# Wider products with v in a two-layer streaming encoder, with embedding products kept in memory meanwhile and first weights split two blocks ahead

## The chip, the core and the metric

The kernel runs on one core of a Trainium2 chip. The metric is the time of one execution on the device in microseconds (us); the median of several runs is compared. The core has a matrix engine (TensorE, "PE" in the profile, with "PEld" for its weight loads), a vector engine (VectorE, "DVE"), a scalar engine (ScalarE, "ACT"), a general engine (GpSimd, "POOL") and a queue that issues transfers (SyncE, "SP"). Each works through its own instructions strictly in the order written. TensorE writes its results to a small memory of accumulators, PSUM; the other data lie in the on-chip memory SBUF, and inputs and outputs lie in the chip's large memory.

## What is computed

Two request groups, 512 prompt frames and 32 sample frames, run through the same two layers; the kernel lays them side by side as 544 columns. Per layer:

```python
u = x @ w_in                       # 13 pieces: q,k,v,z of branch A; q,k,v,z of B; x,z of C; 3 gates
ya = band_attention(qa, ka, va)    # softmax over the frame's chunk of 64 and up to 8 chunks before it
yb = retention(rope(qb), rope(kb), vb); yc = rg_lru(conv(xr))
merged = sum of sigmoid(g_b) * ((y_b * silu(z_b)) @ w_branch[b]) over the three branches
r = ALPHA * x + merged @ w_out
r = r + sigmoid(r @ w_ple_gate) * (pe @ w_ple)     # pe: per-layer embedding input
x = layer_norm(r)
```

Two pieces matter here. In the attention of branch A, with 8 heads of 64 features, the softmax weights of a head are multiplied by v. And `pe @ w_ple`, called the embedding products below, is needed only at the end of a layer.

## The kernel before

Everything is feature-major: 128 features on the partitions, 544 frames along the free dimension, four such tiles in one "slab" of SBUF. There are 15 slabs in a pool that all large intermediate results share, and a slab that is free again is given to the next tile that asks for one.

**Weights in blocks.** A unit is a 128-feature slice of one product, such as `("pl", 3)` or `("wo", 0)`; it consists of 2, 4 or 8 blocks of 128 x 128 weights. `UNITS` (line 60) lists them in the order they run: the embedding products `pl` first, then x of the convolution, v, q and k of attention, the pieces of retention, the three branches, then `wo` (w_out) and `pg` (w_ple_gate). Numbers are kept at full precision by splitting each operand in a high and a low part: ACT copies a weight tile to a rounded high part (`split`, L209) and DVE subtracts to get the low part (L210). A block (L254) is then three products, high x high, high x low, low x high, each over 288 and 256 columns: six matmuls.

**The order of work.** The program is one list per engine, written out by hand. Each block is preceded by a `tick`, which raises a clock by one, calls `stream()` and lets waiting jobs (generators that yield a number of ticks) take their next step. `stream(lead)` splits the weights of all blocks up to `lead` blocks ahead of the present one, four blocks at a time; each second split of a chunk of eight blocks frees a landing buffer (there are three) and issues the load of a later chunk on the SP queue (L201). At the very start two transfers bring the embedding input, four the input x; ACT and DVE split them (`hilo`, L262 and L263). PE runs dummy products (`busy(WARM)`, L269) until its first operands are there. `evac` takes the accumulators of a unit to SBUF; for `pl` this is one ACT copy of 544 columns (L931) into a slab, `env["ple", 0]` or `env["ple", 1]`. Two accumulators serve all units in turn (`ps_mm`), so a unit can start only when the copy of the unit two before it is done.

**Attention of the prompt.** Heads go in pairs; a pair `p` takes three steps, `qs` = (0,1), (2,) and (3,), where each number is a block of 128 queries, which sees i+1 blocks of keys. `attn_step` first calls `flush()`, which issues the products with v that earlier steps left in `env["pvs"]`, then the scores (L402), the exponentials (L353 on DVE, L355 on ACT) and their division by the sum (L359, L360), then transposes the result on PE (L418) block by block and copies it back over itself (L419, ACT). Last it leaves its own product with v for a later flush. `attn_pv` (L432) has one product per block of queries, block of keys and head: 64 rows of output, 128 columns. A step begins every 8 ticks and ends 14 ticks after its start. The output of a pair goes to `ya` by a DVE copy (L437).

**End of a layer.** `gate` (L951 to L954) multiplies the sigmoid of the `pg` product by the embedding product, which has lain in its two slabs since the start of the layer. In the first layer `split_ahead` meanwhile splits weights of the second into slabs of their own.

Of the kernel before, what the change touches and what calls it, by code (L numbers as in the profile page):

```python
# [64 lines left out]
LEAD = 8  # L65

HELD = (6, 2)
WARM = 16

PACE = {  # L70
# [53 lines left out]
def encoder(ctx: ExitStack, tc, xT, pT, W, RB, KC, VC, PAR, CST, LGB, o_y, o_k, o_v, o_rp, o_rs, o_cv, o_lr):  # L124
# [9 lines left out]
    sm = pool("sm", 6)  # L134
    qs = pool("qs", 1)
    PS = bass.MemoryType.PSUM
    ps_mm = pool("ps_mm", 2, space=PS)
    ps_sc = pool("ps_sc", 2, space=PS)
    ps_tp = pool("ps_tp", 1, space=PS)
# [32 lines left out]

    def tick():
        clock[0] += 1
        stream()
        for j in list(jobs):
            while j[1] <= clock[0]:
                d = next(j[0], None)
                if d is None:
                    jobs.remove(j)  # L180
                    break
                j[1] = clock[0] + d
# [98 lines left out]

    def ple_split(l):
        pr, p2 = ple_in[l]
        for k in range(2):
            hilo(p2[:, k], p2[:, 2 + k], pr[:, k])

    V.memset(zero.bitcast(F32), 0.0)
    busy(WARM)
# [32 lines left out]
    def layer(l, env, nxt):  # L321
# [40 lines left out]
        def attn_job():  # L362
            while not all(k in env for k in ("vatok", "gates", ("K", 0))):
                yield 2
            env["ya"] = sl("ya")
            env["pvs"] = []
            bias_loads(0)
            yield 4
            for p in range(4):
                while ("K", p) not in env:  # L370
                    yield 2
                for j in range(2):
                    G.memset(env["bias", p, j][0:64, 448:512], NEG)
                for qs in ((0, 1), (2,), (3,)):
                    if qs[0] == 2 and p < 3:
                        bias_loads(p + 1)
                    add(attn_step(p, qs))
                    yield PACE["step"]
            yield PACE["attn_end"]
            flush()  # L380
            env["ya1"] = True
# [6 lines left out]
        def attn_step(p, qs):  # L388
            QTh, QTl, KTh, KTl = (env[k] for k in ("QTh", "QTl", "KTh", "KTl"))
            flush()  # L390
            scs, xs, todo = [psum("sc") for _ in range(2)], [], []
            o = 0
            now = [], []

            for j in range(2):
                xs.append(tmp("sx", (128, 512)))
            for i in qs:
                n = (i + 1) * 128
                for k, (q_, k_) in enumerate(((QTh, KTh), (QTl, KTh), (QTh, KTl))):
                    for j in range(2):  # L400
                        r = slice(64 * j, 64 * j + 64)
                        T.matmul(scs[j][:, o:o + n], lhsT=q_[r, p, i * 128:i * 128 + 128], rhs=k_[r, p, :n],  # L402
                                 start=k == 0, stop=k == 2)
                for j in range(2):
                    now[j].append((xs[j][:, o:o + n], scs[j][:, o:o + n], env["bias", p, j][:, 512 - n:]))
                o += n
            for j in range(2):
                for a in todo:
                    norm(*a)
                todo = [exps(*a) for a in now[j]]  # L410
                yield PACE["at1"]
            for a in todo:
                norm(*a)
            yield PACE["at2"]
            for j in range(2):
                tp = psum("tp")
                for c in range(0, o, 128):
                    T.transpose(tp[:, c:c + 128], xs[j][:, c:c + 128], ident)  # L418
                copy("p%d" % j)(xs[j][:, :o], tp[:, :o])  # L419
                yield PACE["at3"]  # L420
            env["pvs"].append(lambda: attn_pv(p, qs, xs))

        def attn_pv(p, qs, xs):
            if qs[0] == 0:
                env["pv"] = psum("pv")
            pv = env["pv"]
            o = 0
            for i in qs:
                for kt in range(i + 1):
                    for j in range(2):  # L430
                        h = 2 * p + j
                        T.matmul(pv[64 * j:64 * j + 64, i * 128:i * 128 + 128],  # L432
                                 lhsT=env["vatok"][:, kt, h * 64:h * 64 + 64], rhs=xs[j][:, o:o + 128],
                                 start=kt == 0, stop=kt == i)
                    o += 128
            if qs[-1] == 3:
                copy("pv")(env["ya"][:, p, :NP], pv)  # L437

        def sample_loads():
            t = sl("kvc", shape=(128, 4 * N))  # L440
# [404 lines left out]
        def evac(kind, t, ps, hf=None):  # L845
# [36 lines left out]
            elif kind == "xr":  # L882
                if t == 0:
                    env["xrp"] = xrp = sl("xrp", shape=(128, 4, N + 6))
                    V.memset(xrp[:, :, 0:3], 0.0)
                    V.tensor_copy(xrp[:, :, NP + 3:NP + 6], pa[:, P_SC:P_SC + 12].rearrange("p (a b) -> p a b", a=4))
                xrp = env["xrp"]
                S.copy(xrp[:, t, 3:3 + NP], pv[:, :NP])
                S.copy(xrp[:, t, NP + 6:], pv[:, NP:])  # L889
                if t == 3:  # L890
                    Q.dma_start(out=o_cv[l, :, :, 0:3], in_=xrp[:, :, NP:NP + 3])
                    Q.dma_start(out=o_cv[l, :, :, 3:6], in_=xrp[:, :, NP + NS + 3:NP + NS + 6])
                add(lru_tile(t), PACE["lt00"] if t == 1 else PACE["lt0"])
            elif kind in ("za", "zb", "zc"):
                for f in {"za": ("ya1", "ya2"), "zb": ("yb",), "zc": ("yc",)}[kind]:
                    need(env, f)
                y = env["y" + kind[1]]
                if t == 0:
                    env[kind] = (sl(kind + "h", F32R), sl(kind + "l", F32R))
                h, lo = env[kind]  # L900
                z = tmp("z")
                S.activation(z, pv, AF.Sigmoid)  # L902
                if kind == "zb":
                    V.scalar_tensor_tensor(z, pv, pcol(P_GN, t), z, MUL, MUL)
                else:
                    V.tensor_tensor(z, pv, z, MUL)
                V.tensor_tensor(z, z, y[:, t], MUL)
                hilo(h[:, t], lo[:, t], z)
            elif kind[0] == "g":
                sg = tmp("sg")  # L910
                S.activation(sg, pv, AF.Sigmoid)  # L911
                env["sg", t] = sg
            elif kind[0] == "b":
                sg = env.pop(("sg", t))
                a, b = t // 4, t % 4
                if kind == "bC":
                    if b == 0:
                        env["m", a] = sl("m")
                    V.tensor_tensor(env["m", a][:, b], pv, sg, MUL)
                else:  # L920
                    V.tensor_tensor(sg, pv, sg, MUL)  # L921
                    m = env["m", a][:, b]
                    (V if kind == "bB" and t == 7 else G).tensor_tensor(m, m, sg, ADD)  # L923
                    if kind == "bB":
                        if b == 0:
                            env["mh", a], env["ml", a] = sl("mh", F32R), sl("ml", F32R)
                        hilo(env["mh", a][:, b], env["ml", a][:, b], m)
            elif kind == "pl":
                if t % 4 == 0:
                    env["ple", t // 4] = sl("ple")  # L930
                S.copy(env["ple", t // 4][:, t % 4], pv)  # L931
            elif kind == "wo":
                a, b = t // 4, t % 4
                if b == 0:
                    env["r", a] = sl("r")
                r, xh_, xl_ = env["r", a][:, b], st["xh"][a][:, b], st["xl"][a][:, b]
                V.scalar_tensor_tensor(r, xh_.bitcast(F32), ALPHA, pv, MUL, ADD)
                V.scalar_tensor_tensor(r, xl_.bitcast(F32), ALPHA, r, MUL, ADD)  # L938
                hilo(xh_, xl_, r)
            elif kind == "pg":  # L940
                if t == 7 and hf and l == L - 1:
                    for _ in gate(t, ps, hf):
                        pass
                else:
                    add(gate(t, ps, hf), 0)
# [39 lines left out]
        for group in UNITS:  # L985
            kind, t = group[0]
            if kind == "wg":
                at["use"] += 8
                at["more"] = 0
                continue  # L990
            if l + 1 < L and kind == "wo" and t == 3:
                add(split_ahead(l))
            if l + 1 == L and kind == "pg" and t == 0:
# [44 lines left out]

    with tc.manual_schedule():
        envs = [{} for _ in range(L + 1)]  # L1040
        stream(2)
        ple_split(0)
        add(x_job(envs[0]), PACE["x"])
        for l in range(L):
            layer(l, envs[l], envs[l + 1])
        while jobs:
            tick()
# [81 lines left out]
```

## Time and profile before

| | |
|---|---|
| median of 3 runs | 1309.77 us (1309.71 to 1310.03) |
| profiled execution | 1309.81 us, its span 1308.0 us |
| PE busy | 1291.7 us of the span |
| DVE, ACT, POOL busy | 717.3, 546.1, 177.0 us |
| bytes moved | 125.90 MB, mean 96 GB/s |
| largest group | L254, blocks of weights: 84% of the chain that ended last |

All views come from one profiled execution. A row of the timeline begins with the start in us and the length in us, then engine, line, operation, the tiles written and read, shapes and a count (x6); in square brackets stands the idle time before it and what ended it. A length covers the whole of merged instructions, with the tail of the last, so PE's spacing is better read from starts. A full-precision product (f32, not the split kind) leaves two records on PE for each matmul. The chain is the work that ended last, followed back from the end.

### The profile page before, as it was taken

The page shows a single profiled execution, that of the slowest core. Times are in us where ns is not written, and L with a number is a line of the kernel's source. Part 1 is how long each engine was busy: PE and PEld are TensorE (multiplying, and loading weights), DVE is VectorE, ACT ScalarE, POOL GpSimd, SP SyncE. Part 2 cuts the span into 40 slices and gives each one's busy share as a digit, 9 for nine tenths or more (in the row PEclk, how much of TensorE's full clock was granted, in tenths as well). Part 3 has the DMA queues.
Part 4 walks back from the last instruction along what each step waited for, and adds up shares of the span by engine and source line. Part 5 has one row for each costly group of instructions (what it writes and reads, how often), then busy time and mean ns, then how long its engine had stood idle before and what let it go on. Part 6 is the DMA issues. An engine that isn't in the chain of part 4 may idle for free.

```text
span 1308.0 us, 25456 instructions
## 1 busy us (share of the span) xinstructions
PE 1291.7 (99%) x10744; PEld 1263.5 (97%) x10744; DVE 717.3 (55%) x1271; ACT 546.1 (42%) x1065; POOL 177.0 (14%) x158
## 2 busy tenths in 40 slices
PE   9999999999999999999999999999999999999996
PEld 9999999999999999999989998999999999999996
DVE  5666662573753453465584756626637444434567
ACT  6665544323632232333277655443235322332231
POOL 0210120410101201000032201224001011010000
PEclk9999999999999999999999999999999999999998
DMA  7233522231222222224112335222222222222231
GB/s 282 66 131 98 171 69 80 85 105 50 85 93 82 97 68 94 97 97 146 65 49 66 131 99 166 74 83 82 89 66 81 95 83 86 92 81 97 81 113 69
DMA packets 43457, 125.90 MB, mean 96 GB/s; under 512 B 9360, under 2 KB 11664, under 8 KB 42576
## 3 DMA queue, kind: packets, MB, share of 16 engines
q1 hardware_dynamic: 43344, 124.29, 28.8%
q8 instruction: 84, 1.38, 0.4%
q14 instruction: 29, 0.24, 0.1%
HBM read 112.57 MB, written 7.24 MB: 92 GB/s over the span
## 4 chain that ended last, share of the span: by engine, by line
PE 95%; DVE 3%; DMA 1%; ACT 1%; issue 0%; SPq 0%; POOL 0%; DVEq 0%
PE mm L254 84%; PE pv L432 2%; PE sc L402 2%; PE tp L418 1%; PE tp L330 1%; DMA raw<-in_W 1%; PE sc L661 1%; PE pv L684 1%; PE pv L516 0%; DVE r L813 0%; PE sc L516 0%; DVE xl L263 0%; PE sc L744 0%; PE sc L597 0%; PE pv L679 0%
## 5 line engine op out<-in xcount | busy, mean ns | idle before, releaser
L254 PE MATMUL mm<-xh,wh 128*128 128x288 f32 x2144 | 455.5, 294 | 0.4 <-ACT xrp L889 0.4
L254 PE MATMUL mm<-xh,wl 128*128 128x288 f32 x2144 | 444.1, 288 | 0.0
L254 PE MATMUL mm<-xl,wh 128*128 128x288 f32 x2144 | 442.7, 288 | 0.0
L210 DVE TENSOR_TENSOR wl<-raw,wh 128x512 fp32r<-128x512 f32 (+1 forms) x354 | 261.4, 756 | 283.8 <-ACT wh L209 279.9
L254 PEld LDWEIGHTS mm<-xh,wh 128*128 128x128 f32 x2144 | 328.3, 189 | 10.7 <-issue 7.4
L254 PEld LDWEIGHTS mm<-xl,wh 128*128 128x128 f32 x2144 | 328.8, 188 | 0.0
L254 PEld LDWEIGHTS mm<-xh,wl 128*128 128x128 f32 x2144 | 328.5, 188 | 0.2 <-DVE wl L210 0.2
L209 ACT CAST wh<-raw 128x512 fp32r<-128x512 f32 (+1 forms) x354 | 208.3, 614 | 36.9 <-PE mm L254 30.8
L911 ACT ACTIVATE sg<-mm 128x544 f32<-128x544 f32 x48 | 30.1, 626 | 154.1 <-PE mm L254 154.1
L923 POOL TENSOR_TENSOR m<-m,sg 128x544 f32<-128x544 f32 x30 | 46.8, 1560 | 316.6 <-DVE sg L921 316.6
L355 ACT ACTIVATE sx<-sx,sst 128x128 f32<-128x128 f32 (+4 forms) x68 | 38.0, 559 | 70.1 <-DVE sst L353 66.0
L254 PE MATMUL mm<-xh,held 128*128 128x288 f32 (+1 forms) x320 | 64.0, 291 | 0.3 <-ACT ple L931 0.3
L254 PE MATMUL mm<-ml,wh 128*128 128x288 f32 (+1 forms) x256 | 52.9, 288 | 0.0
L254 PE MATMUL mm<-mh,wl 128*128 128x288 f32 (+1 forms) x256 | 52.6, 286 | 0.0
L254 PE MATMUL mm<-mh,wh 128*128 128x288 f32 (+1 forms) x256 | 52.5, 286 | 0.0
L254 PEld LDWEIGHTS mm<-xh,held 128*128 128x128 f32 x320 | 51.3, 188 | 0.6 <-ACT ple L931 0.5
L254 PE MATMUL mm<-xl,held 128*128 128x288 f32 (+1 forms) x160 | 46.4, 290 | 0.5 <-DVE xl L263 0.5
L262 ACT CAST xh<-r 128x544 fp32r<-128x544 f32 (+2 forms) x32 | 17.0, 532 | 67.8 <-DVE r L938 63.6
L921 DVE TENSOR_TENSOR sg<-mm,sg 128x544 f32<-128x544 f32 x32 | 23.2, 725 | 36.7 <-PE mm L254 36.7
L565 POOL TENSOR_TENSOR swap<-swap,cst 128x544 f32<-128x544 f32 x16 | 25.3, 1580 | 109.8 <-DMA swap<-QB 68.1
L902 ACT ACTIVATE z<-mm 128x544 f32<-128x544 f32 x24 | 15.0, 626 | 59.2 <-PE mm L254 59.1
L254 PEld LDWEIGHTS mm<-mh,wl 128*128 128x128 f32 x256 | 39.3, 188 | 0.0
(251 smaller groups left out, 1791.9 us busy)
## 6 DMA issues: line engine op xcount, KB each, us to landing
raw<-in_W SPq DMA_DIRECT2D x189, 512.0 KB, 3.3
bias<-in_RB SPq DMA_DIRECT2D x16, 256.0 KB, 4.1
x<-in_xT SPq DMA_DIRECT2D x4, 544.0 KB, 9.2
o_v<-VA SPq DMA_DIRECT2D x2, 1088.0 KB, 5.1
o_k<-KT SPq DMA_DIRECT2D x2, 1088.0 KB, 5.1
swap<-KB SPq DMA_DIRECT2D x32, 68.0 KB, 2.0
swap<-QB SPq DMA_DIRECT2D x32, 68.0 KB, 2.0
o_y<-tk SPq DMA_DIRECT2D x6, 256.0 KB, 2.1
```

Of the source, the lines that this page charges most:

```text
L209: S.copy(h[:, k:k + step], t)
L210: V.tensor_tensor(lo[:, k:k + step], t, h[:, k:k + step].bitcast(F32), SUB)
L254: T.matmul(ps[:, MM0 + a:MM0 + b], lhsT=w[:, n % 4, :], rhs=x[:, a:b], start=first and i == 0, stop=last and i == 2)
L262: S.copy(h, src)
L355: S.activation(x, x, AF.Exp, bias=s[:, 0:1], scale=-1.0, accum_out=s[:, 1:2])
L402: T.matmul(scs[j][:, o:o + n], lhsT=q_[r, p, i * 128:i * 128 + 128], rhs=k_[r, p, :n], start=k == 0, stop=k == 2)
L432: T.matmul(pv[64 * j:64 * j + 64, i * 128:i * 128 + 128], lhsT=env["vatok"][:, kt, h * 64:h * 64 + 64], rhs=xs[j][:, o:o + 128], start=kt ...
L565: G.tensor_tensor(sw, sw, cst[:, C_SIN:C_SIN + N], MUL)
L902: S.activation(z, pv, AF.Sigmoid)
L911: S.activation(sg, pv, AF.Sigmoid)
L921: V.tensor_tensor(sg, pv, sg, MUL)
L923: (V if kind == "bB" and t == 7 else G).tensor_tensor(m, m, sg, ADD)
```

## The change

- **Products with v.** The transposed softmax weights no longer overwrite the tile they came from. `env["PT"]` is two slabs, one for each head of a pair, 4 blocks of keys x 512 queries. The copy after the transposes puts each 128 x 128 block in its place there: in the step (0,1) this takes two copies for each head in place of one. `attn_pv` runs once for a pair, after its third step, as four products for each head with 512, 384, 256 and 128 columns. The first step of a pair waits one tick longer before its transposes, so that it comes behind the products of the pair before it.
- **Embedding products.** After the fourth and the eighth of them the full slab is stored to memory (`env["pled"]`), and the slab is free. Before the first `wo` unit two slabs are asked for, and two transfers on the SP queue bring the products back.
- **First weights.** In the first eight ticks `stream` looks two blocks ahead in place of eight; `stream(2)` before the first tick becomes `stream(1)`. In the first layer the first half of the embedding input is split in two pieces, 288 and 256 columns.
- **Dummy products.** 14 in place of 16.

```diff
-WARM = 16
+WARM = 14
...
+    dr = pool("dr", 2, space=bass.MemoryType.DRAM)
...
     def tick():
         clock[0] += 1
-        stream()
+
+        stream(LEAD if clock[0] > 8 else 2)
...
         for k in range(2):
-            hilo(p2[:, k], p2[:, 2 + k], pr[:, k])
+            for a, b in SPANS if l == 0 and k == 0 else ((0, N),):
+                hilo(p2[:, k, a:b], p2[:, 2 + k, a:b], pr[:, k, a:b])
...
             env["pvs"] = []
+
+            env["PT"] = [sl("PT", shape=(128, 4, 512)) for _ in range(2)]
...
-            yield PACE["at2"]
+
+            yield PACE["at2"] + (qs[0] == 0)
+            assert qs[0] or not env["pvs"]
             for j in range(2):
                 tp = psum("tp")
                 for c in range(0, o, 128):
                     T.transpose(tp[:, c:c + 128], xs[j][:, c:c + 128], ident)
-                copy("p%d" % j)(xs[j][:, :o], tp[:, :o])
+                c = 0
+                for i in qs:
+                    copy("p%d" % j)(env["PT"][j][:, :i + 1, i * 128:i * 128 + 128],
+                                    tp[:, c:c + 128 * (i + 1)].rearrange("p (a b) -> p a b", b=128))
+                    c += 128 * (i + 1)
                 yield PACE["at3"]
-            env["pvs"].append(lambda: attn_pv(p, qs, xs))
-
-        def attn_pv(p, qs, xs):
-            if qs[0] == 0:
-                env["pv"] = psum("pv")
-            pv = env["pv"]
-            o = 0
-            for i in qs:
-                for kt in range(i + 1):
-                    for j in range(2):
-                        h = 2 * p + j
-                        T.matmul(pv[64 * j:64 * j + 64, i * 128:i * 128 + 128],
-                                 lhsT=env["vatok"][:, kt, h * 64:h * 64 + 64], rhs=xs[j][:, o:o + 128],
-                                 start=kt == 0, stop=kt == i)
-                    o += 128
             if qs[-1] == 3:
-                copy("pv")(env["ya"][:, p, :NP], pv)
+                env["pvs"].append(lambda: attn_pv(p))
+
+        def attn_pv(p):
+            pv = psum("pv")
+            for kt in range(4):
+                for j in range(2):
+                    h = 2 * p + j
+                    T.matmul(pv[64 * j:64 * j + 64, kt * 128:], lhsT=env["vatok"][:, kt, h * 64:h * 64 + 64],
+                             rhs=env["PT"][j][:, kt, kt * 128:], start=kt == 0, stop=kt == 3)
+            copy("pv")(env["ya"][:, p, :NP], pv)
...
                 S.copy(env["ple", t // 4][:, t % 4], pv)
+                if t % 4 == 3:
+                    env["pled", t // 4] = dr.tile([128, 4, N], F32, tag="ple%d" % (t // 4), name="pled")
+                    Q.dma_start(out=env["pled", t // 4], in_=env.pop(("ple", t // 4)))
...
+            if kind == "wo" and t == 0:
+                for a in range(2):
+                    env["ple", a] = sl("ple")
+                    Q.dma_start(out=env["ple", a], in_=env["pled", a])
...
-        stream(2)
+        stream(1)
```

## The prediction

> **What bounds the kernel now.** I read the page's busy times first, then the chain that ended last, then the stretches which the change touches.
>
> ```profile
> PE 1291.7 (99%) x10744; PEld 1263.5 (97%) x10744; DVE 717.3 (55%) x1271; ACT 546.1 (42%) x1065; POOL 177.0 (14%) x158
> ```
>
> ```profile
> PE 95%; DVE 3%; DMA 1%; ACT 1%; issue 0%; SPq 0%; POOL 0%; DVEq 0%
> PE mm L254 84%; PE pv L432 2%; PE sc L402 2%; PE tp L418 1%; PE tp L330 1%; DMA raw<-in_W 1%; PE sc L661 1%; PE pv L684 1%; PE pv L516 0%; DVE r L813 0%; PE sc L516 0%; DVE xl L263 0%; PE sc L744 0%; PE sc L597 0%; PE pv L679 0%
> ```
>
> PE is the bound from its first product to near the end. So time is won in two ways only: PE gets less to do, or it waits less. The attention of the first layer (95 to 211 us) has no wait at all:
>
> ```profile
> 95.00:211.00 116.00, 116.00 (x1040) 107.08 (x1039) 71.60 (x192) 59.22 (x144) 16.89 (x21) 1.00 0.36 112
> ```
>
> The columns are stretch, length, then busy time and count of PE, PEld, DVE, ACT and POOL. DVE and ACT have 44 and 57 us to spare there, so what the change adds to them has cover, and what it takes from PE is won in full.
>
> **Products with v.** Here is one group of them between its neighbours, then, from the chain, the last group of the layer, two other full-precision groups and a long run of blocks. That run gives 264.42 / 2106 = 0.126 us for a matmul of a block and 0.75 for a block.
>
> ```profile
> 110.23 0.49 PE L418 MATMUL tp<-cst,sx 128*128 128x128 f32 x3
> 110.65 0.88 PE L432 MATMUL pv<-sx,vatok 128*64 128x128 f32 x12
> 111.45 0.50 PE L402 MATMUL sc<-KTh,QTh 64*128 64x512 f32 x2
> ```
>
> ```profile
> 208.82 1.68 PE pv L432 x28
> ...
> 230.95 1.08 PE sc L597 x32
> ...
> 290.57 1.02 PE pv L684 x16
> ...
> 349.73 264.42 PE mm L254 x2106
> ```
>
> ```profile
> L597 PE MATMUL sc<-vbtok,kbtok x128: 222/222/271, 230.9 to 887.1; 128*64 128x64 f32 x128
> ```
>
> ```profile
> L684 PE MATMUL pv<-inner,vbtok x128: 272/273/324, 290.5 to 966.3; 128*64 128x128 f32 x128
> ```
>
> A product leaves two records, and the two heads of a pair run side by side in the two halves of the array, so two records are one slot. 12 records (6 slots) take 111.45 - 110.65 = 0.80 us, 28 records (14 slots) 1.68. The difference, 0.88 over 8 slots, gives 0.11 us for a slot of 128 columns; what is left, 0.80 - 0.66 = about 0.15, is the price of a group, however long it is (changing over from another kind of product and back, and the first weight load that nothing hides).
>
> What will a slot of 512 columns cost? No row of before has a full-precision product over 128 columns. The L597 and L684 rows answer it nearest: 16 slots of 64 columns take 1.08, 8 slots of 128 columns 1.02. Both stream 1024 columns. Half as many instructions with the same columns save 0.06 us: the columns are the price, some 0.85 ns each in a slot, and a slot less is worth at most 0.06 / 8 = 7 ns. So fusing products saves almost nothing by itself.
>
> Count then. A pair has 20 slots now (10 blocks, two records) of 128 columns, 2560 columns; afterwards 2 x (512 + 384 + 256 + 128) = 2560 columns in 8 slots. Streaming goes from 20 x 0.109 = 2.18 us to 2.18 - 12 x 0.002 to 12 x 0.007, that is 2.10 to 2.16; for eight pairs -0.2 (I take it, near the low end, since 0.109 us for 128 columns at 0.833 ns leaves 2 ns of its own) to -0.7 us. Groups: a step ends 14 ticks after its start and steps begin every 8, so each flush finds one group, except the last, which finds two (the 28 records above are 12 + 16). That makes 11 a layer, 22 in all; after the change one for a pair, 8. 14 x 0.15 = **-2.1 us**. Together -2.1 to -2.8; I take **-2.3**.
>
> What this adds: 16 more ACT copies (two for 128 and 256 columns in place of one for 384) at under 0.5 us each, 8 us over two stretches with about 57 us free each. One tick (0.75 us, a block) more of delay in a first step lies inside a pair's 24 ticks; the products of the pair before come at tick 9 of the pair, the first copy into `PT` behind transposes at tick 10, so ACT waits for no product. The last flush is longer (16 records of 2.3 us for 1.68), which delays `ya1` by 0.6 us and is already in the count.
>
> **The start.** The profile's first microseconds, PE, ACT, DVE, SP:
>
> ```profile
> 1.20 4.00 PE L269 MATMUL mm<-zero 128*128 128x272 f32 x16 [1.20 <-DVE eps L289]
> 5.29 1.52 PE L254 MATMUL mm<-phl,wh 128*128 128x288 f32 x4
> ...
> 8.93 0.41 PE L254 MATMUL mm<-phl,wl 128*128 128x288 f32 x2
> 10.05 0.52 PE L254 MATMUL mm<-phl,wh 128*128 128x288 f32 x2 [0.71 <-ACT ple L931]
> ```
>
> ```profile
> 4.59 1.30 ACT L262 CAST phl<-pr 128x544 fp32r<-128x544 f32 x2
> 7.62 0.71 ACT L209 CAST wh<-raw 128x256 fp32r<-128x256 f32 x2 [1.74 <-DMA raw<-in_W]
> 8.87 0.62 ACT L209 CAST wh<-raw 128x512 fp32r<-128x512 f32 x1 [0.53 <-DMA raw<-in_W]
> 9.40 1.12 ACT L931 COPY ple<-mm 128x544 f32<-128x544 f32 x2
> 10.40 0.63 ACT L209 CAST wh<-raw 128x512 fp32r<-128x512 f32 x1
> 10.92 0.66 ACT L262 CAST xh<-x 128x544 fp32r<-128x544 f32 x1
> ```
>
> ```profile
> 654.88 0.43 ACT L262 CAST xh<-r 128x288 fp32r<-128x288 f32 x1 [0.19 <-DVE r L813]
> ```
>
> ```profile
> 9.52 0.69 DVE L210 TENSOR_TENSOR wl<-raw,wh 128x512 fp32r<-128x512 f32 x1 [0.70 <-ACT wh L209]
> ```
>
> PE waits twice. First for the split input: 4.59 + 0.65 (half of 1.30) = 5.24, product at 5.29. A cast of 288 columns takes 0.43, so the first product comes at 5.07; the low part too is ready sooner. I put block 1 at 0.3 us ahead. The dummies then end at about 4.7 (two of 0.25 less), before they are in the way. Second, PE stands from about 9.2 to 10.05 since ACT, in its strict order, waits for the weights of blocks 4 and 8 (7.62, 8.87) ahead of the copy that frees the accumulator (9.40). With two blocks of lead that copy stands ahead of both casts: it comes right after block 1, at about 7.6 to 8.2, the cast for block 4 to 8.8 (its first half at 8.5), and unit 2 starts when block 3 ends, at 8.9 in place of 10.05: **1.15 us** ahead.
>
> Then it gives some back. The x cast now stands in front:
>
> ```profile
> 3.07 0.43 SPq L297 DMA_DIRECT2D x<-in_xT  x1
> ```
>
> ```profile
> DMA to landing us min/median/max: 7.1/9.2/9.7
> ```
>
> x lands at 3.07 + 7.1 = 10.2 at the earliest. ACT's list is: x cast to 10.85, copy of unit 2 to 11.35, cast for block 8 to 11.9, DVE's low part to 12.6. PE wants block 8 at 8.9 + 4 x 0.75 = 11.9 and its low part 0.5 later, 12.4. So a wait of 0.2, with its restart 0.3, arises there. Sum of the start: -1.15 + 0.3 = **-0.9 us**. Its ends: -1.2 without the new wait, and 0 where the cast for block 8 comes another ACT step or two later (0.5 to 0.65 each). That `stream(1)` stands for `stream(2)` changes nothing: both split exactly four blocks.
>
> **The embedding products in memory.** Four stores and four loads of 1.1 MB. On SP, a store waits for an ACT copy; behind it in the queue stand the weight loads, each of which waits for a cast later in ACT's own order, so the queue loses only the issue, 0.4 us. The transfer itself is another matter in the first layer:
>
> ```profile
> 10.00:15.00 5.00, 4.95 (x39) 4.95 (x40) 2.74 (x5) 4.38 (x9) 0.00 (x0) 1.00 1.02 411
> 15.00:20.00 5.00, 5.00 (x41) 4.88 (x39) 3.64 (x6) 4.45 (x10) 0.00 (x0) 1.00 0.71 258
> 20.00:25.00 5.00, 5.00 (x40) 4.95 (x40) 4.16 (x10) 3.40 (x9) 0.00 (x0) 1.00 0.32 100
> 25.00:30.00 5.00, 5.00 (x42) 5.00 (x41) 2.25 (x10) 1.03 (x2) 0.00 (x0) 1.00 1.00 407
> 30.00:35.00 5.00, 4.97 (x40) 4.76 (x39) 2.10 (x5) 3.86 (x8) 0.00 (x0) 1.00 0.41 147
> ```
>
> The last two columns are the transfer engines' share and GB/s: full up to 15 us and again from 25 to 30. Two stores at 411 GB/s are 5.4 us of work; 15 to 25 us has 1.45 + 3.4 = 4.9 free. So weight loads land some 3 us later at the start. They have the cover: a load is issued when a chunk three ahead has been split, 20 blocks (15 us) before its own first split, and usually takes 3.3:
>
> ```profile
> raw<-in_W SPq DMA_DIRECT2D x189, 512.0 KB, 3.3
> ```
>
> So 0, and likewise for the loads before `wo`, 5.4 us of transfer against 15 - 3.3 = 11.7. Their slabs: at that point 4 (x) + 4 (`mh`, `ml`) of 15 are taken, so seven are free, most for long; the last, `m`, is read in the copies of the unit just before. Attention has 2 slabs more for `PT` and 2 fewer for embedding products. From `wo` on the count is as before. Cost 0; without the cover, up to 5 us (below).
>
> **Sum.** The profiled execution took 1309.81, 0.04 above the median of 1309.77. 1309.8 - 2.3 - 0.9 = **1306.6**; on the median 1306.5.
>
> **Rivals.**
> 1. *The start gives its gain back:* the cast for block 8, now only two blocks ahead, comes 1.2 us late. For it: its cover is 1.5 us of product time against 0.5 + 0.6 + 0.7 of copy, cast and subtraction. Against it: the copy ahead of it waits for nothing new. 1309.8 - 2.3 = 1307.5.
> 2. *The clock comes later.* The dummies take 0.25 us for 272 columns, twice the 0.126 of a later product; the first four products (1.52 in the row at 5.29) are still slow, so the rate changes at about 6.6. With two dummies less PE idles from 4.7 to 5.07. If the slow stretch (from 1.20) repeats, half of 5.4 us is lost: 1309.3. Against it: the idle time before the first product, 0.3 us now, grows by 0.1 to 0.2 only, and the waits behind it shrink. The Trainium skill ("TensorE: Matmul & The Clock Gate", Part 1) has a free-running window of about 3.4 us that decides by activity; a delay of one such window would be an estimated 1.7 us by that page, 1308.3.
> 3. *Long products are cheap.* If the weight loads set the slot of 128 columns and not its columns, 512 columns at the block's rate (288 columns in 0.126) would take 0.22: 2 x (0.22 + 0.17 + 0.11 + 0.11) = 1.2 us a pair for 2.16, another 7.5 us in all, 1299. Against it stand L597 and L684: same weights, half the columns, half the slot. The Trainium skill (same page, "Back-to-back issue gap") has such a rule: streams of 128 columns at 81 ns, of 512 at 131, hence far less for each column. By it, an estimate, eight products of 320 columns on average at 106 ns for twenty at 81 would halve the 17.4 us of streaming: 1298. The L597 and L684 rows speak against it here.
> 4. *Slower: stores starve the first weights.* Place: 17 to 35 us, where the constants fill the engines already. Price: if stores run at the pace of the outputs of equal size (5.1 us each),
>
> ```profile
> o_v<-VA SPq DMA_DIRECT2D x2, 1088.0 KB, 5.1
> ```
>
> and hold the loads behind them, those land 10 us later; cover is 11.7 less the 3 us worked out above. From then on each us is PE's: some 5 us, 1309.8 - 3.2 + 5 = 1311.6. It decides from 9 us of delay.
> 5. *The change doesn't do what it says:* groups fall away, but PE then waits in attention for DVE's exponentials. Only the start is left, 1308.9. Against it: 116.00 of 116.00 busy.
>
> **Chances.** Forecast 0.62 (own range 1305.5 to 1307.4), rival 1 0.16, rival 2 0.05, rival 3 0.03, rival 4 0.08, rival 5 0.06. The range 1304.6 to 1309.3 leaves out rivals 3 and 4 and the tails. A difference under 0.2% (2.6 us) can't be told from none with this kernel; that line is at 1307.15. Faster: most of the forecast (0.53), some of rival 1 (0.06), rival 3: 0.62. Slower: rival 4 and what I have not seen, 0.10. The same: 0.28.
>
> **What would show it.** L432 with 128 records for 320, in 8 groups, of 2.3 us from the first start to the next scores. The first L254 at about 5.07, unit 2 near 8.9 with no wait for `ple L931`, a short one near 11.9 for `wh L209` or `wl L210`. The first split product of x (`mm<-xh`) 0.9 us sooner than before. PE still 116 of 116 in attention. A wait of PE for weights between 20 and 45 us, or near the loads of `ple`, would make it wrong; so would a PE group of L432 well under 2 us.

## The result and the profile after

| | median | runs |
|---|---|---|
| before, beside the runs of after | 1309.91 us | 1309.71 to 1310.07 |
| after | 1319.74 us | 1319.02 to 1320.99 |

The ratio is 1.0076, 95% interval 1.0063 to 1.0089: the change makes the kernel **slower by about 10 us**. The prediction said 1306.5 with a range to 1309.3, so its direction was wrong. Lines moved by 2 to 10: blocks of weights are L256 now (L254), products with v L441 (L432), transposes of the softmax weights L426 (L418), the copies behind them L429 (L419), exponentials L357 and L359 (L353, L355). The profiled execution took 1319.02 us.

The page of after, busy time, and from its chain one group of products with v, all eight of a pair in one go:

```profile
PE 1294.9 (98%) x10550; PEld 1259.8 (96%) x10550; DVE 719.1 (55%) x1272; ACT 546.6 (41%) x1082; POOL 174.6 (13%) x158
```

```profile
187.71 2.30 PE pv L441 x16
```

The groups are as forecast: eight, of 2.30 us. Worked out from starts, L441 holds PE for 18.43 us in the whole run, L432 held it for 20.79. The loss is elsewhere. Here is what PE waited for in after (total, times, longest), the first and third of them new:

```profile
PE tp L481 <- ACT PT L429: 4.3, 2, 2.2
PE tp L750 <- DVE r L963: 2.0, 2, 1.4
PE tp L426 <- ACT PT L429: 1.5, 2, 0.8
```

In the windows, after the stretch stand PE busy and count, then PEld, DVE, ACT, POOL, and then the granted clock, the third number from the end:

```profile
95.00:211.00 116.00, 113.02 (x917) 101.79 (x916) 71.45 (x190) 58.45 (x150) 15.53 (x21) 0.99 0.35 113
...
162.00:166.00 4.00, 1.83 (x15) 1.59 (x14) 3.39 (x8) 1.13 (x4) 1.51 (x2) 1.00 0.36 131
166.00:169.50 3.50, 3.50 (x18) 3.17 (x18) 0.69 (x1) 1.87 (x5) 0.00 (x0) 0.51 0.08 20
169.50:215.00 45.50, 45.50 (x387) 40.68 (x386) 24.29 (x58) 20.08 (x49) 8.72 (x10) 1.00 0.23 70
818.00:821.50 3.50, 3.44 (x16) 3.38 (x17) 0.23 (x1) 1.66 (x5) 0.00 (x0) 0.51 0.01 2
```

Attention stood at 116.00 of 116.00 before; now 3 us of it are idle, and the idle time is followed by a stretch at **half clock** (0.51 in the row of 166.00): 18 records in 3.5 us, where the 0.126 us of a matmul of a block make 28. The clock's records in the trace give it as 3.41 us from 166.09, and again 3.41 us from 818.03, in the second layer's attention; before has none between 6.60 and 1300. So a layer loses 0.8 + 2.2 us of waits and 3.41 / 2 = 1.7 of pace, 4.7 us.

Where the wait comes from stands in the timeline. First before, the last head of a pair's first step, then after at the same place:

```profile
159.81 0.49 PE L418 MATMUL tp<-cst,sx 128*128 128x128 f32 x3
...
160.34 0.48 ACT L419 COPY sx<-tp 128x384 f32<-128x384 f32 x1 [0.20 <-PE tp L418]
...
162.40 0.49 PE L475 MATMUL tp<-cst,sx 128*128 128x128 f32 x3
...
162.96 0.62 ACT L355 ACTIVATE sx<-sx,sst 128x384 f32<-128x384 f32 x1 [2.14 <-DVE sst L353]
```

```profile
160.25 1.29 POOL L576 TENSOR_TENSOR KB<-KB,cst 128x512 f32<-128x512 f32 x1 [7.41 <-DVE KB L573]
...
160.34 1.75 DVE L212 TENSOR_TENSOR wl<-raw,wh 128x512 fp32r<-128x512 f32 x1 [0.21 <-ACT wh L211]
...
161.31 0.49 PE L426 MATMUL tp<-cst,sx 128*128 128x128 f32 x3
...
162.16 1.35 POOL L571 TENSOR_TENSOR swap<-swap,cst 128x544 f32<-128x544 f32 x1
162.20 1.53 DVE L364 TENSOR_SCALAR sx<-sx,sst 128x384 f32<-128x384 f32 x1
...
163.65 0.55 DVE L357 CUSTOM_DVE_ANT_0 sx<-sc,bias 128x384 f32<-128x384 f32 x1
...
164.30 0.61 ACT L359 ACTIVATE sx<-sx,sst 128x384 f32<-128x384 f32 x1 [3.99 <-DVE sst L357]
...
164.91 0.52 ACT L429 COPY PT<-tp 128x128 f32<-128x128 f32 x2
...
165.24 0.42 DVE L364 TENSOR_SCALAR sx<-sx,sst 128x384 f32<-128x384 f32 x1
...
165.48 0.55 PE L481 MATMUL tp<-cst,sx 128*128 128x128 f32 x3 [2.17 <-ACT PT L429]
```

Before, the copy L419 is done at 160.8, ahead of the next step's exponentials; those wait 2.14 us for DVE, and nobody needs ACT meanwhile. After, the transposes come one tick later, and with that the copies stand *behind* the next step's exponentials in ACT's list. By the code, the second head's transposes of a pair's first step come 3 + 3 + 2 + 3 = 11 ticks after the step's start, and the second head's exponentials of the next step 8 + 3 = 11 ticks after it; on the same tick the older job goes first, and one tick more turns the order round. The exponentials wait 3.99 us for DVE, and the copy waits with them, though its data lie ready from 161.8. The copy frees the only accumulator for transposes, and the sample's attention job (L481) needs that one next: PE stands.

DVE is late for its own reason: its division of 128x384 values takes 1.53 us beside POOL's product (162.16) and 0.42 without it (165.24). Just before, its subtraction of 128x512 values takes 1.75 us beside another product of POOL (160.25); at the start of before it took 0.69 (L210 at 9.52). The Trainium skill ("SBUF — State Buffer", Who interferes with whom) lets VectorE and GpSimd share one pair of ports under an exclusive lock, the only conflict among engines that it knows; these rows agree with it. That the wait would be shorter without POOL's products is argued here, and no run tries it.

The first product now, the casts of the first weights in before and in after, and the rows of the stored products:

```profile
1.20 3.54 PE L271 MATMUL mm<-zero 128*128 128x272 f32 x14 [1.20 <-DVE eps L293]
5.33 1.41 PE L256 MATMUL mm<-phl,wh 128*128 128x288 f32 x4 [0.59 <-ACT phl L264]
```

```profile
3.76 0.71 ACT L209 CAST wh<-raw 128x256 fp32r<-128x256 f32 x2 [1.54 <-DMA raw<-in_W]
```

```profile
4.18 0.71 ACT L211 CAST wh<-raw 128x256 fp32r<-128x256 f32 x2 [1.97 <-DMA raw<-in_W]
```

```profile
pled<-ple SPq DMA_DIRECT2D x4, 1088.0 KB, 4.9
ple<-pled SPq DMA_DIRECT2D x4, 1088.0 KB, 7.2
```

The landing of the first weights released ACT's cast at 4.18 us (before: 3.76), the first product came at 5.33 and the full clock at 9.07 (before: 6.60).

### The profile page after: what moved, and what is told of

It reads as the page before. It is cut to its first block, busy times and chain, and to the rows that moved or that the text cites. A ratio compares the mean times of both kernels' runs of the same rounds, so it can differ in the third digit from the quotient of the medians.

```text
span 1317.2 us, 25083 instructions
## 1 busy us (share of the span) xinstructions
PE 1294.9 (98%) x10550; PEld 1259.8 (96%) x10550; DVE 719.1 (55%) x1272; ACT 546.6 (41%) x1082; POOL 174.6 (13%) x158
## 4 chain that ended last, share of the span: by engine, by line
PE 80%; DVE 5%; ACT 2%; issue 1%; DMA 0%; DVEq 0%; POOL 0%; ACTq 0%
PE mm L256 72%; PE tp L426 1%; PE pv L441 1%; PE sc L408 1%; DVE wl L212 1%; PE tp L334 1%; PE sc L667 1%; PE pv L690 1%; DVE xl L265 0%; PE sc L750 0%; DVE r L819 0%; PE sc L603 0%; DVE lru_i L555 0%; PE pv L685 0%; PE sc L494 0%
## 5 line engine op out<-in xcount | busy, mean ns | idle before, releaser
L256 PE MATMUL mm<-xh,wh 128*128 128x288 f32 x2144 | 457.0, 294 | 0.4 <-ACT xrp L895 0.4
L256 PE MATMUL mm<-xh,wl 128*128 128x288 f32 x2144 | 445.0, 289 | 0.0
L256 PE MATMUL mm<-xl,wh 128*128 128x288 f32 x2144 | 443.8, 288 | 0.0
L256 PEld LDWEIGHTS mm<-xh,wh 128*128 128x128 f32 x2144 | 328.9, 189 | 10.8 <-issue 7.5
L256 PEld LDWEIGHTS mm<-xl,wh 128*128 128x128 f32 x2144 | 329.7, 188 | 0.0
L256 PEld LDWEIGHTS mm<-xh,wl 128*128 128x128 f32 x2144 | 329.6, 189 | 0.0
L359 ACT ACTIVATE sx<-sx,sst 128x128 f32<-128x128 f32 (+4 forms) x68 | 38.1, 560 | 82.0 <-DVE sst L357 67.8
L256 PE MATMUL mm<-xh,held 128*128 128x288 f32 (+1 forms) x320 | 64.0, 291 | 0.3 <-ACT ple L937 0.3
L256 PE MATMUL mm<-mh,wl 128*128 128x288 f32 (+1 forms) x256 | 53.1, 289 | 0.0
L256 PE MATMUL mm<-mh,wh 128*128 128x288 f32 (+1 forms) x256 | 53.1, 289 | 0.0
L256 PE MATMUL mm<-ml,wh 128*128 128x288 f32 (+1 forms) x256 | 52.8, 288 | 0.0
L256 PEld LDWEIGHTS mm<-xh,held 128*128 128x128 f32 x320 | 51.3, 188 | 0.6 <-ACT ple L937 0.5
L256 PE MATMUL mm<-xl,held 128*128 128x288 f32 (+1 forms) x160 | 46.5, 290 | 0.7 <-DVE xl L265 0.7
L256 PEld LDWEIGHTS mm<-mh,wh 128*128 128x128 f32 x256 | 39.3, 189 | 0.0
```

What stands on the lines that cost most here:

```text
L256: T.matmul(ps[:, MM0 + a:MM0 + b], lhsT=w[:, n % 4, :], rhs=x[:, a:b], start=first and i == 0, stop=last and i == 2)
L359: S.activation(x, x, AF.Exp, bias=s[:, 0:1], scale=-1.0, accum_out=s[:, 1:2])
```

## The experiments

Ratios are against before, timed on the same chip in turn.

**The tick taken out of after.** The step now issues the products itself, ahead of its own transposes.

```diff
-            yield PACE["at2"] + (qs[0] == 0)
+            yield PACE["at2"]
+            if qs[0] == 0:
+                flush()
```

> The changed kernel without the extra tick: the first step of a pair calls flush itself, right before its transposes, so that the products of the pair before stand ahead of its copies; all else is kept. Theory T (the tick puts the copies into PT behind the exponentials of the next step in ACT's order, PE waits for the transposes' accumulator, and the long waits halve its clock): the waits of 0.8 and 2.17 us and half of 3.41 us of slow clock go away in both layers, 2 x 4.7 = 9.4 us, so 1319.7 - 9.4 = about 1310.3 (1309.3 to 1311). Rival R1 (the copies in two pieces and the long groups of products delay the copies, tick or not): 1318 to 1320, with the waits of PE for PT still there.

Measured: 1309.27 us, ratio 0.9999 (0.9989 to 1.0008), at the lower end of what the theory of the tick expected. Attention has no idle time, and the clock stays at 1.00:

```profile
95.00:211.00 116.00, 116.00 (x950) 103.54 (x950) 72.18 (x192) 59.59 (x152) 15.52 (x21) 1.00 0.37 111
```

The tick costs the whole 10 us. But nothing of the forecast gain of 3.2 us is seen either; the later runs look for it.

**The tick alone, in before.**

```diff
-            yield PACE["at2"]
+            yield PACE["at2"] + (qs[0] == 0)
```

> The kernel before with nothing but the extra tick in the first step of a pair. T: PE waits for the copy of the transposed tiles as in the changed kernel, twice 0.8 and twice 2.2 us, and the clock drops to half for some 3.4 us behind each long wait: 1309.9 + 9.4 = about 1319 (1316 to 1321). R1: no change, 1309.5 to 1310.5.

Measured: 1317.2 us, ratio 1.0053 (1.0038 to 1.0068). One tick by itself, with the old products and one copy for each head, gives the same waits on the same lines:

```profile
PE tp L475 <- ACT sx L419: 3.6, 2, 2.0
...
PE tp L418 <- ACT sx L419: 1.6, 2, 0.8
```

So neither the two copies nor the long groups make them. L475 and L418 are L481 and L426 of after. Only the wait of 2.0 us was followed by half clock (3.41 us from 165.67); the other, of 1.6 us, was not.

**After with the old start.**

```diff
-WARM = 14
+WARM = 16
...
-        stream(LEAD if clock[0] > 8 else 2)
+        stream()
...
-            for a, b in SPANS if l == 0 and k == 0 else ((0, N),):
+            for a, b in ((0, N),):
...
-        stream(1)
+        stream(2)
```

> The changed kernel with the start as before: 16 dummy products, weights split eight blocks ahead from the first tick, the embedding input split whole. If the new start is worth nothing or a little less than nothing (first product of x at 19.43 us against 19.08), 1319.7 - 0.35 = 1319.4 (1318.9 to 1320). If the late clock of the profiled execution (9.07 against 6.60 us) comes from the two dummies and hides a gain of 0.9, the clock is at 6.6 again and the time about the same; if the start is what costs the 9 us, 1311.

Measured: 1317.86 us, ratio 1.0057 (1.0042 to 1.0072), with the same waits and both stretches of half clock. The start isn't the cause of the 10 us. The time lies under the 1318.9 to 1320 that were expected if the start is worth nothing, and 1.9 us under after; the intervals of the two ratios overlap, so whether the new start cost after something stays open. (The 19.08 us in the expectation are the start of a weight load; the first split product of x came at 19.19 in before and 19.43 in after.)

**The sample's job two ticks later**, in after.

```diff
-    "va0": 5, "va": 3, "step": 8, "attn_end": 9, "at1": 3, "at2": 2, "at3": 3, "sample": 11, "sa1": 4, "sa2": 4,
+    "va0": 5, "va": 3, "step": 8, "attn_end": 9, "at1": 3, "at2": 2, "at3": 3, "sample": 13, "sa1": 4, "sa2": 4,
```

> After, with the extra tick, but the sample's attention job starting two ticks later (13 for 11). If the long waits (2.17 us, and the half clock that follows for 3.41 us) arise only since the sample's transposes need the one accumulator that the first step's late copy holds, they are gone: about 1319.7 - 2 x (2.17 + 1.7) = 1312, with the two waits of 0.8 us of the step's own transposes left and no stretch of half clock. If the strict order of ACT makes whatever comes next wait, the wait only changes its line: 1317 to 1320, with half clock again.

Measured: 1314.02 us, ratio 1.0035 (1.0023 to 1.0047). Half clock is gone, and the waits are shorter:

```profile
PE tp L426 <- ACT PT L484: 2.8, 4, 0.8
...
PE tp L426 <- ACT PT L429: 1.6, 2, 0.9
```

Both theories had a part of it: the long wait goes, but the next user of the accumulator, the step's own transposes behind the sample's copy (L484), waits in its place, four times up to 0.8 us. The waits add up to 4.4 us, about what the run lost against before (4.25). In after they add up to 5.8 us and half clock to 3.4.

**The embedding products in memory alone**, in before: only the store and the reload of the change.

```diff
+                if t % 4 == 3:
+                    env["pled", t // 4] = dr.tile([128, 4, N], F32, tag="ple%d" % (t // 4), name="pled")
+                    Q.dma_start(out=env["pled", t // 4], in_=env.pop(("ple", t // 4)))
...
+                    env["ple", a] = sl("ple")
+                    Q.dma_start(out=env["ple", a], in_=env["pled", a])
```

> The kernel before with nothing but the embedding products stored to memory and loaded back before wo. If the transfers are hidden: 1309.9 (1309.5 to 1310.3). If they or the other order of the slabs cost what grows between the two attentions in the changed kernel (shift 4.1 us at 217 us, 4.9 at 679): 1310.6. If the stores starve the first weights (rival 4 of the prediction): 1311 to 1315, with PE waiting for wh or wl between 20 and 45 us.

Measured: 1311.15 us, ratio 1.0010 (1.0001 to 1.0020): it costs some 1.4 us. Between 20 and 45 us PE waits for nothing, so the first weights were not starved (rival 4). PE's waits in the whole run explain only 0.4 of the 1.4 us (7.0 us together for 6.6). Set instruction beside instruction, another 0.7 us builds up in `wo` (0.2 in the first layer, 0.5 in the second), whose products read `mh` and `ml`: they follow one another at 125.5 ns where before has 124.6. Some 0.3 us are left without a name. In the last 35 us of the second layer's `wo`, PE busy throughout at full clock, first before, then this kernel (stretch, PE busy and count, clock, transfers):

```profile
1200.00:1235.00 35.00, 35.00 (x284) 1.00 0.27 91
```

```profile
1200.00:1235.00 35.00, 35.00 (x281) 1.00 0.37 135
```

**Other slabs for `mh` and `ml`, in before.** Nothing goes to memory; one slab more is taken and let go ahead of each pair, so that the two are handed other slabs. (The traces hold no addresses; that the slabs differ follows from the edit.)

```diff
+                            skip = sl("skip")
+                            G.memset(skip[:, 0, :1], 0.0)
                             env["mh", a], env["ml", a] = sl("mh", F32R), sl("ml", F32R)
```

> Before, with one slab more taken and let go ahead of each pair mh, ml (one POOL memset of a single column each, four in all), so that mh and ml lie in other slabs, and nothing else changed: no products once for a pair, no store. In before the products of mh and ml follow one another at 124.6 ns on average, in every kernel with the embedding products in memory at 125.4 to 125.8, over 768 matmuls a run. Theory: the place of the data in SBUF sets that pace, so it moves here too, somewhere between 124.5 and 126.0 ns, most likely to 125.5 or more, and the time by up to +0.8 us (768 x 1.1 ns). Rival: the transfers of the reload or its queue slow PE: the pace stays 124.6 and the time that of before within 0.3 us.

Measured: 1310.84 us, ratio 1.0007 (0.9998 to 1.0016); the pace is 125.5 ns here too, without any added transfer:

```profile
1200.00:1235.00 35.00, 35.00 (x280) 1.00 0.28 91
```

The time alone can't be told from no change, but the pace can: 768 x 0.9 ns = 0.7 us, half of what the memory step cost, comes without any transfer. So the place of the data is enough to make this half. Which property of the place does it, no run shows.

**The start alone**, in before: the start's edits of the change.

```diff
-WARM = 16
+WARM = 14
...
-        stream()
+        stream(LEAD if clock[0] > 8 else 2)
...
-            hilo(p2[:, k], p2[:, 2 + k], pr[:, k])
+            for a, b in SPANS if l == 0 and k == 0 else ((0, N),):
+                hilo(p2[:, k, a:b], p2[:, 2 + k, a:b], pr[:, k, a:b])
...
-        stream(2)
+        stream(1)
```

> Before with the new start alone (two blocks of lead in the first eight, the split input of block 1 in two parts, 14 dummies for 16). The prediction's sum gives -0.9 us: first product at 5.07, the first split product of x (mm<-xh) at 18.2 for 19.08, 0.9998 to 0.9990 of before in time. Rival, from the profile of after, where the first raw weights landed at 4.18 for 3.73 and the full clock came at 9.07 for 6.60: the gain depends on when the first weights land and on where the clock changes, and on average nothing is left: -0.3 to +0.4 us, with an early and a late kind of execution that lie up to 1.7 us apart.

Measured: 1309.10 us, ratio 0.9994 (0.9986 to 1.0003), 0.7 us less, but with no change inside the interval. In this execution the first weights landed early (ACT's first cast of them started at 3.47 us), the first product came at 4.78, full clock at 4.43, and the wait for `ple` shrank from 0.7 to 0.3:

```profile
4.78 1.21 PE L254 MATMUL mm<-phl,wh 128*128 128x288 f32 x4
```

**Products and memory, without tick and new start.**

```diff
-WARM = 14
+WARM = 16
...
-        stream(LEAD if clock[0] > 8 else 2)
+        stream()
...
-            for a, b in SPANS if l == 0 and k == 0 else ((0, N),):
+            for a, b in ((0, N),):
...
-            yield PACE["at2"] + (qs[0] == 0)
+            yield PACE["at2"]
+            if qs[0] == 0:
+                flush()
...
-        stream(1)
+        stream(2)
```

> After without the extra tick and with the start of before: what is left is the products once for a pair (-2.35 us measured in the groups of L441) and the embedding products in memory (+1.4 us measured alone). If the two add up: 1309.7 - 2.35 + 1.4 = about 1308.8, with the attention stretches 1.1 us shorter each and some 0.5 to 0.7 us lost after each of them. If the products' gain is a feature of the records only and does not reach the end: 1310 to 1311. No wait for PT in either theory.

Measured: 1310.62 us, ratio 1.0004 (0.9995 to 1.0013), 1.8 us above what the two parts were to add up to. Two things are missing. First, the attention of each layer got only 0.7 us shorter, for 1.17 in the groups themselves. PE's time of the first layer's attention, from start to next start, worked out from the trace (before, this kernel, difference in us):

```
blocks of weights, 710 records     93.05  93.33  +0.27
products with v                    10.39   9.22  -1.17
transposes of softmax weights       8.68   8.85  +0.17
scores                             10.00  10.01  +0.01
all the rest                        5.50   5.50   0.00
```

A block ahead of a group of products with v takes 0.19 us more than its six matmuls, ahead of transposes 0.09; transposes behind such a group take 0.48 for 0.42. Before, the groups stood between transposes and scores, where these prices were paid anyway; with three groups among blocks 0.44 us a layer are given back. Second, in this execution one load of weights at the end of the first layer landed 4.8 us after its issue (before: 3.3): fifteen of its sixteen parts were there after 3.3 us, and one came 1.5 us later. ACT waits for it in its order, with the sigmoid of `gate` behind it, and PE waits for that 1.6 us:

```profile
614.16 0.61 ACT L211 CAST wh<-raw 128x512 fp32r<-128x512 f32 x1
621.23 0.62 ACT L211 CAST held<-raw 128x512 fp32r<-128x512 f32 x1 [6.46 <-DMA raw<-in_W]
...
622.28 0.61 ACT L962 ACTIVATE sg<-mm 128x544 f32<-128x544 f32 x1
```

```profile
624.62 0.33 PE L752 MATMUL sc<-cst,r 128*128 128x128 f32 x1 [1.64 <-DVE r L965]
```

The same wait is 1.2 to 2.1 us in three more of the profiled kernels with the products in memory, where again one part alone came 1.0 to 1.8 us after the rest; it is 0.2 to 0.5 in others (0.2 also with the other slabs alone), and not seen in before. Whether the change makes this load late more often stays open.

**Without the tick, 16 dummies.** The kernel of the first experiment, and:

```diff
-WARM = 14
+WARM = 16
```

> After without the extra tick (the step flushes before its own transposes) and with the 16 dummies of before, new start otherwise. If two dummies less let the clock change a window (3.4 us) later in some executions, this one is up to 1.7 us faster than the same kernel with 14 dummies in those, and its full clock always comes at about 5.5 to 6.6: -0.5 to -1.5 us against before. If the dummies make no difference: as the kernel with 14, about -0.5 us against before (1309.27 beside 1309.72).

Measured: 1309.82 us, ratio 1.0001 (0.9992 to 1.0010): as with 14. Full clock came at 5.91.

**Without the tick, other slabs.** The kernel of the first experiment, and:

```diff
+                            skip = sl("skip")
+                            G.memset(skip[:, 0, :1], 0.0)
                             env["mh", a], env["ml", a] = sl("mh", F32R), sl("ml", F32R)
```

> After without the extra tick and with the same one slab more ahead of each pair mh, ml. If the place sets the pace, it differs from the 125.7 ns of the kernel without the extra slab, by up to 1.2 ns either way, and the time by up to 0.8 us to either side of that kernel's 1309.3. If transfers set it, 125.4 to 125.8 as before and the same time. In both, no wait for PT, and the attention stretches as in that kernel.

Measured: 1308.65 us, ratio 0.9992 (0.9983 to 1.0001), the lowest ratio of all, 1.25 us under before, at the edge of what can be told from no change. The pace of these products went from 125.7 to 124.8 ns: placement works both ways.

```profile
1200.00:1235.00 35.00, 35.00 (x283) 1.00 0.41 146
```

The profiled execution, 1311.45, was the longest of its eleven: full clock at 9.83, and the late load above. The wait behind that load is as long as those that halved the clock in attention, and yet the clock stayed full:

```profile
625.74 0.33 PE L752 MATMUL sc<-cst,r 128*128 128x128 f32 x1 [2.12 <-DVE r L967]
```

The clock's records tell why. In every profiled execution the time between two changes of the clock, the last included, is a whole number of stretches of 3.413 us: in after 46, 1, 190, 1 and 143 of them. So each execution has a fixed grid of such stretches. Here are, from the windows, two stretches of after's grid, the wait in the first of them, then two of this kernel's (stretch, PE busy and count, clock, transfers):

```profile
162.67:166.09 3.42, 1.25 (x11) 1.00 0.42 153
166.09:169.50 3.41, 3.41 (x17) 0.50 0.08 20
```

```profile
620.82:624.23 3.41, 2.80 (x23) 1.00 0.00 0
624.23:627.64 3.41, 1.90 (x16) 1.00 0.11 12
```

After's wait lies within one stretch, which has 2.17 us of idle time; here the grid cuts the wait into 0.61 and 1.51. Worked out from PE's records over all thirteen profiled executions, the stretch ahead of each of the 18 drops to half clock (five in attention, one near the end of each execution) had 1.76 us of idle time or more, and no other stretch at full clock had more than 1.70.

**The same with 16 dummies.**

```diff
-WARM = 14
+WARM = 16
```

> After without the extra tick, with the other slabs for mh and ml, and with 16 dummies for 14. With 14 dummies that kernel's executions lay at 1308.0 to 1308.7 or some 1.5 us above (profiled: full clock only at 9.83 us). If the two dummies less are what lets the clock come a window of 3.4 us later, this one has no late executions: full clock at 5.4 to 6.6 us, 1308.0 to 1308.8 throughout, 0.999 of before. If the number of dummies does not decide it, executions 1.5 us above the best are as frequent as with 14.

Measured: 1309.68 us, ratio 1.0000 (0.9991 to 1.0009), 1309.1 to 1311.4, and full clock only at 10.41 in the profiled execution. So the number of dummies does not decide it. What the executions with late full clock share is the idle time ahead of the first product:

```profile
1.20 4.00 PE L271 MATMUL mm<-zero 128*128 128x272 f32 x16 [1.20 <-DVE eps L293]
5.69 1.41 PE L256 MATMUL mm<-phl,wh 128*128 128x288 f32 x4 [0.49 <-ACT phl L264]
```

0.49 here, 0.55 and 0.59 in the two others with 9.83 and 9.07; under 0.1 in before. The kernel with products and memory and the old start stood 0.43 us there and had its full clock at 5.40 all the same, since the same grid decides: 5.40 is the end of a stretch, and only 0.21 of the 0.43 us lay ahead of it. In each of the thirteen executions full clock came at the end of the first stretch in which PE was idle for 0.34 us or less; 0.49, 0.55 and 0.59 us put it off by one stretch. That is 3.41 us more at half clock, 1.7 us. Where the grid lies at the start differs from one profiled execution to the next.

## Why the prediction was wrong

**What bounds the kernel.** Right for before: PE, with no wait in attention. Its own test, "PE still 116 of 116 in attention", is what failed: 113.02.

**The tick** is the step that failed: "One tick (0.75 us, a block) more of delay in a first step lies inside a pair's 24 ticks", and from the order of the products and copies, "so ACT waits for no product". That compares the copies with the products of the pair before, the wait that the tick was to avoid, and takes the 57 us that ACT is free as cover. It does not ask what else stands at the new place in ACT's list. There stand the exponentials of the next step, which wait up to 4 us for DVE, and behind the copy an accumulator that exists once and is wanted next by another job. Before with the tick alone: +7.5 us; after without it: -10 us. No rival named it. Rival 5 came nearest, with PE waiting in attention for DVE's exponentials, but it only took back the gain of the groups (1308.9), and neither the tick nor the copy was in it. The rival that was slower put its loss at the start (stores that starve the first weights), and from 20 to 40 us, where these would be missed, PE is busy for 19.97 of 20 us in after, as before but for 0.01.

**Half clock** was considered for the start alone. In after it makes 3.4 of the 10 us, by the prediction's own price, half of 3.41 us each time. The Trainium skill ("TensorE: Matmul & The Clock Gate", Part 1) has a free-running window of 3413 ns that decides the clock; the grid of 3.413 us in the clock's records agrees with it. Its rule to avoid idle gaps of over about 3 us (Why this matters for your kernels) does not hold here as a limit, and the measurement decides: 2.03 to 2.19 us of idle time within one stretch were enough five times, and 2.12 us cut by the grid into 0.61 and 1.51 were not.

**Products with v.** The mechanism and the size were right for the groups themselves: 18.43 for 20.79 us, -2.36 for a forecast -2.3, columns as the price, and the rival of cheap long products refuted. As a term of the whole time it was too large by what it left out: the price of a group depends on its neighbours, and where the groups stand among blocks a layer's attention gets 0.72 us shorter, -1.45 us for both.

**The start.** -0.9 was forecast, -0.7 measured alone, with the interval on both sides of nothing, so the gain is not shown. The wait for `ple` became shorter, as forecast. In the profiled execution of after the gain was lost again, by the rival of the later clock: 9.07 for 6.60. That rival's own doubt, that the idle time ahead of the first product grows by 0.1 to 0.2 us only, is what failed there: it was 0.59.

**Embedding products in memory** were costed at 0 and measured 1.4 us (0.1 to 2.6). No wait of PE for the first weights came of the transfers, as argued; that slabs handed out in another order change PE's pace (0.7 us) was not thought of.

**The sum of after**: 1309.81 + 5.8 (waits) + 3.4 (half clock) - 2.36 (groups) + 1.4 (memory) + 0.24 (its start, by the first product of x) = 1318.3, for 1319.02 measured; 0.7 us are left without a name, of the size of the neighbours' prices. The terms come from different kernels, so the sum is an estimate.

## What to carry to other kernels

Where engines keep a written order, free time on an engine is no cover for an instruction that is moved: list what stands ahead of it at its new place, what that waits for, and who needs next the buffer that it frees. A buffer that exists once ties together jobs that share no data, so a move of one tick in one of them is to be checked against all of its users. And a wait is worth more than its length where the clock answers it: 2.2 us of idle time within one stretch of the clock's grid cost 3.9 here.

## What the runs showed of the hardware

- The clock changed only on a grid of 3.413 us, which lies elsewhere in each execution. A stretch with 1.76 us or more of PE's idle time was followed by half clock, 18 times out of 18; one with 1.70 or less never was, in thirteen profiled executions. A wait of 2.12 us that the grid cut into 0.61 and 1.51 left the clock full.
- At the start, full clock came behind the first stretch with 0.34 us or less of idle time; 0.49, 0.55 and 0.59 us put it off by one stretch.
- DVE's division of 128x384 values took 1.53 us beside a POOL product and 0.42 without.
- The pace of the same products, with no wait and at full clock, was 124.6, 125.5, 125.7 or 124.8 ns in kernels that hand other slabs to their moving operands. It stayed the same to 0.1 ns in kernels that give out the slabs alike.
- In four executions one load of 512 KB had fifteen of its sixteen parts landed 3.3 us after its issue, and the last came 1.0 to 1.8 us later.
